# Order-only dependences that put weight splits behind the layer norms, in an fp32 encoder kernel

## Chip, cores and metric

The kernel runs on one core of one Trainium2 chip. The metric is device time in microseconds: 1150.9 us, the median of three runs (1150.8 to 1151.14).

## What is computed

A two-layer encoder over 256 tokens of width 1024, in fp32. Cut to its skeleton:

```python
x = layer_norm(x, emb_ln_g, emb_ln_b)
for l in range(2):
    h = hybrid_mixer(x, ...)            # w_in (1024 x 7680), two attentions, a short convolution, gates, w_mix_out
    x = layer_norm(alpha * x + h, ln_g[l, 0], ln_b[l, 0])
    h = memory_cross_attention(x, mem, ...)   # xa_q, xa_kv (on mem), xa_o
    x = layer_norm(alpha * x + h, ln_g[l, 1], ln_b[l, 1])
    h = conv_ffn(x, ...)                # ffn_w_in (1024 x 5632), convolution, SiLU, ffn_w_out (2816 x 1024)
    x = layer_norm(alpha * x + h, ln_g[l, 2], ln_b[l, 2])
```

So there are seven layer norms: one at the start and three in each layer. Each needs whole rows of the residual, and the next projection needs its result.

## The kernel before

**Weight units.** All weights come as units of 128 x 1024 fp32 numbers (512 KB), in the order in which they are used. `prefetch` (L1063 to L1070) keeps `LOOK = 7` units ahead of the step that is being written: a DMA on SyncE's queue fills a `raw` buffer (four of them), ScalarE rounds it to fp32r (`hi`, the copy of L249), VectorE subtracts (`lo = raw - hi`, L250). `hi` and `lo` have eight buffers each (`WB`). I call the pair of instructions a weight split. A product of two split operands is three matmuls (`mm3`, L244 to L246): high by high, high by low, low by high; a unit feeds 24 of them where it meets 256 tokens.

**Layer norm.** The tokens stand in two tiles of 128 rows, x[0] (x_133 in the printed order) and x[1] (x_134). `ln_part` (L335 to L347) adds the branch's result from PSUM to the residual (L339) and takes statistics of 256 columns (`bn_stats`, L344). `ln` (L349) has two kinds of steps. `norm`: aggregate the statistics (L357), square root on ScalarE (L358), subtract and multiply by the gain (`sub`, L361), reciprocal (L373), scale and add the bias (`scale`, L366; two pieces of 512 columns for x[0], four of 256 for x[1]). `transp`: TensorE transposes a piece into PSUM (L402), then ScalarE and VectorE split it (`split_from`, L249 and L250) into the activations `xt` that the next projection reads.

**Order.** `interleave` lays the steps in one list by hand-written costs, and fill steps (keys and values of the memory, which need no norm) are put where the main line waits. Within that, SyncE's queue keeps the written order; on the other engines a scheduler orders the instructions by its own estimate when the program is built. Each engine then runs its list in order. The PSUM banks `acc` rotate over three buffers, so the third group of a projection reuses the bank of the last key group, which ScalarE copies out (L425). In the cross attention the keys are split too (L250, from a `big` buffer: the key split).

Of the kernel before, what the change touches and what calls it, by code (L numbers as in the profile page):

```python
# [21 lines left out]
AF = mybir.ActivationFunctionType  # L22
ALU = mybir.AluOpType
AX = mybir.AxisListType

P = 128
# [8 lines left out]
ALPHA = (2.0 * DEPTH) ** 0.25  # L35
NEG = -1.0e30
NOSYNC = mybir.DependencyInfo(mybir.DependencyClass.NoSync, mybir.DependencyReason.DATA)
# [75 lines left out]
def interleave(main, fills, banks):  # L113
# [5 lines left out]
    def emit(s):  # L119
        nonlocal clock, free, nfill  # L120
        while nfill < s.fill:
            nfill += 1
            emit(fills[nfill - 1])
        free -= s.acq
        steps.append(s)
        clock += s.cost
        if s.rel:
            pending.append((clock + s.lat, s.rel))

    while cur is not None or active:  # L130
# [4 lines left out]
        for c in list(active):  # L135
            s = c[3]
            if isinstance(s, Spawn):
                active.append([s.name, c[1] + s.delay, s.gen, next(s.gen)])
                c[3] = next(c[2], None)
                moved = True  # L140
            elif s is None:
                done[c[0]] = c[1]
                active.remove(c)
                moved = True
            elif c[1] <= clock and s.acq <= free:
                emit(s)
                c[1] = clock + s.lat
                c[3] = next(c[2], None)
                moved = True
            if moved:  # L150
                break
# [13 lines left out]
        if isinstance(cur, Step) and cur.acq <= free:  # L165
            emit(cur)
            cur = next(main, None)
            continue
# [25 lines left out]
def rd(t):  # L194
    return t.bitcast(F32)


class Encoder:
# [47 lines left out]
        mm(o, ll, rh, start=False, stop=last)  # L246

    def split_from(self, src, ah, al):
        self.nc.scalar.copy(ah, src)  # L249
        self.nc.vector.tensor_tensor(out=al, in0=src, in1=rd(ah), op=ALU.subtract)  # L250

    def proj_f8(self, u, xa, o):

# [80 lines left out]
    def ln_part(self, i, c, acc=None):  # L334

        nc, x = self.nc, self.x[i]
        sl = slice(*c)
        if acc is not None:
            nc.vector.scalar_tensor_tensor(out=x[:, sl], in0=x[:, sl], scalar=ALPHA, in1=acc,  # L339
                                           op0=ALU.mult, op1=ALU.add)  # L340
        if c[0] == 0:
            self.T["st", i] = self.small(24).rearrange("p (c s) -> p c s", c=4)
        for q in range(c[0] // 256, c[1] // 256):
            nc.vector.bn_stats(self.T["st", i][:, q], x[:, 256 * q:256 * q + 256])  # L344
        if i == 0 and c[0] == 0:

            nc.scalar.activation(self.small(1), self.T["st", 0][:, 0, 0:1], AF.Sqrt, bias=self.epsb, scale=0.0)  # L347

    def ln(self, i, nxt, rel, pre=2.6):  # L349

        st = {}
        w = 512 if i == 0 else 256

        def norm():
            nc, x = self.nc, self.x[i]
            mv, rs = self.small(2), self.small(1)
            nc.vector.bn_aggr(mv, self.T["st", i])  # L357
            nc.scalar.activation(rs, mv[:, 1:2], AF.Sqrt, bias=self.epsb, scale=1.0)  # L358
            def sub(h):
                sl = slice(w * h, w * h + w)  # L360
                return nc.vector.scalar_tensor_tensor(out=x[:, sl], in0=x[:, sl], scalar=mv[:, 0:1],  # L361
                                                      in1=self.lng[:, sl], op0=ALU.subtract, op1=ALU.mult)

            def scale(h):
                sl = slice(w * h, w * h + w)
                nc.vector.scalar_tensor_tensor(out=x[:, sl], in0=x[:, sl], scalar=rs,  # L366
                                               in1=self.lnb[:, sl], op0=ALU.mult, op1=ALU.add)

            if nxt is not None:
                for h in range(D // w):  # L370
                    sub(h)
                    if h == 0:
                        nc.vector.reciprocal(rs, rs)  # L373
                    scale(h)
                return

            n, nb = D // w, self.small(1)
            sub(0)
            nc.vector.reciprocal(rs, rs)
            r = nc.vector.scalar_tensor_tensor(out=nb, in0=mv[:, 0:1], scalar=-1.0, in1=rs,  # L380
                                               op0=ALU.mult, op1=ALU.mult)
            sl = slice(w * (n - 1), D)
            nc.scalar.activation(x[:, sl], x[:, sl], AF.Identity, bias=nb, scale=rs)
            nc.gpsimd.tensor_tensor(out=x[:, sl], in0=x[:, sl], in1=self.lng[:, sl], op=ALU.mult)
            nc.gpsimd.tensor_tensor(out=x[:, sl], in0=x[:, sl], in1=self.lnb[:, sl], op=ALU.add)
            for h in range(n - 1):
                if h:
                    self.tc.add_manual_dep(sub(h).ins, r.ins.name, NOSYNC, reason="order of the last rows")
                scale(h)
            for h in range(n):  # L390
                sl = slice(w * h, w * h + w)
                eng = nc.scalar if h % 2 else nc.sync
                eng.dma_start(self.out[i * P:(i + 1) * P, sl], x[:, sl])

        def transp(h):
            nc, n = self.nc, w // P
            if i == 0 and h == 0:
                self.T[nxt] = self.act_tile()
            a = self.T[nxt]
            pt = self.att()[:, :w].rearrange("p (k t) -> p k t", k=n)  # L400
            for k in range(n):
                nc.tensor.transpose(pt[:, k], self.x[i][:, (n * h + k) * P:(n * h + k + 1) * P], self.ident)  # L402
            t, k = n * h // 4, n * h % 4
            self.split_from(pt, a.his[t][:, k:k + n, i * P:(i + 1) * P], a.los[t][:, k:k + n, i * P:(i + 1) * P])

        yield Step(norm, 0, pre, rel=rel)
        if nxt is not None:
            for h in range(D // w):
                yield Step(lambda h=h: transp(h), 0.11 * w / P, 0.3 if h < D // w - 1 else 1.0, acq=1, rel=1)
# [652 lines left out]
    def prefetch(self, upto):  # L1062
        nc = self.nc  # L1063
        while len(self.split) < min(upto, len(self.order)):
            raw = self.raw()
            nc.sync.dma_start(raw, self.aps["w"][len(self.split)])
            hi = self.wp.tile([P, 1024], F32R, tag="hi", name=self.nm("hi"), bufs=self.WB)
            lo = self.wp.tile([P, 1024], F32R, tag="lo", name=self.nm("lo"), bufs=self.WB)
            self.split_from(raw, hi, lo)
            self.split.append((hi, lo))  # L1070

    def load(self, t, src):
# [41 lines left out]
    @with_exitstack  # L1114
    def emit(ctx, self, tc, aps, out):
        nc, PS = tc.nc, bass.MemoryType.PSUM
        self.nc, self.tc, self.aps, self.out = nc, tc, aps, out
        self.uid, self.split, self.bias = 0, [], {}
        self.cst = ctx.enter_context(tc.tile_pool(name="cst", bufs=1))
        self.wp = ctx.enter_context(tc.tile_pool(name="wp", bufs=4))  # L1120
        self.bigp = ctx.enter_context(tc.tile_pool(name="big", bufs=self.BIG))
        self.tmp = ctx.enter_context(tc.tile_pool(name="tmp", bufs=2))
        self.sm = ctx.enter_context(tc.tile_pool(name="sm", bufs=4))
        self.psa = ctx.enter_context(tc.tile_pool(name="psa", bufs=self.ACC, space=PS))
        self.psb = ctx.enter_context(tc.tile_pool(name="psb", bufs=self.ATT, space=PS))
        with tc.manual_schedule(engines={mybir.EngineType.SP}):
            pos = 0
            for s in self.steps:
                if s.units:
                    pos += len(s.units)  # L1130
                    self.prefetch(pos + self.LOOK)
                s.fn(*self.split[pos - len(s.units):pos])
# [59 lines left out]
```

## Time and profile before

| | |
|---|---|
| median of 3 runs | 1150.9 us |
| the profiled execution | 1151.81 us, span 1150.0 us |
| granted TensorE clock, mean | 0.989 |
| TensorE matmul busy | 1114.6 us (97%) |
| VectorE busy | 799.2 us (69%) |
| ScalarE busy | 614.2 us (53%) |
| weight splits on VectorE | 355, 431.8 us, 1222 ns each |
| weight splits on ScalarE | 355, 370.7 us, 1049 ns each |

The busy times are sums over the whole span. Successive instructions of VectorE and ScalarE overlap by some 0.1 us in the records, so n of them take a little less than n times one. [...]

### The profile page before, as it was taken

Reading aid. Unit: us, or ns where it says so; the run is one execution under the profiler, and the core shown is the slowest. Engines: PE = TensorE matmul, PEld = TensorE weight load, DVE = VectorE, ACT = ScalarE, POOL = GpSimd, SP = SyncE. Lnnn points to the kernel's source line nnn. Section 1 sums busy time; section 2 is a strip of 40 time slices with the busy share of each in tenths; the row PEclk is TensorE's granted clock in tenths of the full one; section 3 lists DMA queues with packets and bytes.
Section 4 is the critical chain, followed back from the end, with each engine's and each line's share of the span. In section 5 each row is a group of like instructions: output and inputs, shape, how many; then the busy total and the mean of one; then the engine's idle time right before and its main releaser. Section 6 shows DMA issues by size and latency. Waiting matters only on the chain.

```text
span 1150.0 us, 20250 instructions
## 1 busy us (share of the span) xinstructions
PE 1114.6 (97%) x8172; PEld 1060.7 (92%) x8172; DVE 799.2 (69%) x1198; ACT 614.2 (53%) x958; POOL 12.4 (1%) x18
## 2 busy tenths in 40 slices
PE   7999999999899899999999999999999979999997
PEld 6999999999898899998889999999989969999986
DVE  7788888567764866665586888865696675766644
ACT  6656776444553565554445666654555445555531
POOL 0000000000000000000000000000000000000001
PEclk9999999999899999999999999999999999999999
DMA  7883536456452555555747544555664443555551
GB/s 293 283 257 129 198 115 216 169 195 206 168 184 98 196 183 184 184 183 183 258 146 224 177 149 165 186 174 188 206 232 150 147 155 133 173 183 184 185 181 37
DMA packets 60478, 208.65 MB, mean 181 GB/s; under 512 B 7008, under 2 KB 8288, under 8 KB 60384
## 3 DMA queue, kind: packets, MB, share of 16 engines
q1 hardware_dynamic: 59952, 206.83, 52.7%
q8 instruction: 64, 1.05, 0.4%
q10 hardware_dynamic: 432, 0.52, 0.1%
q14 instruction: 30, 0.25, 0.1%
HBM read 204.18 MB, written 1.05 MB: 178 GB/s over the span
## 4 chain that ended last, share of the span: by engine, by line
PE 68%; DVE 3%; ACT 1%; issue 1%; DMA 0%; DVEq 0%; ACTq 0%
PE acc L245 19%; PE acc L244 19%; PE acc L246 18%; PE att L245 3%; PE att L246 3%; PE att L244 3%; DVE lo L250 1%; PE att L402 1%; DVE x L361 1%; DVE s L344 1%; DVE x L339 0%; DVE x L366 0%; ACT hi L249 0%; DMA raw<-in_w_dram 0%; PE att L603 0%
## 5 line engine op out<-in xcount | busy, mean ns | idle before, releaser
L250 DVE TENSOR_TENSOR lo<-raw,hi 128x1024 fp32r<-128x1024 f32 x355 | 431.8, 1222 | 239.7 <-ACT hi L249 238.1
L249 ACT CAST hi<-raw 128x1024 fp32r<-128x1024 f32 x355 | 370.7, 1049 | 391.4 <-PE acc L245 238.8
L244 PE MATMUL acc<-big,hi 128*128 128x256 f32 x1952 | 556.1, 286 | 3.3 <-ACT big L283 1.7
L245 PE MATMUL acc<-big,hi 128*128 128x256 f32 x1952 | 555.4, 285 | 2.7 <-DVE big L250 2.7
L246 PE MATMUL acc<-big,lo 128*128 128x256 f32 x1952 | 555.3, 285 | 0.2 <-DVE lo L250 0.2
L244 PEld LDWEIGHTS acc<-big,hi 128*128 128x128 f32 x1952 | 375.9, 193 | 5.0 <-ACT big L283 2.1
L245 PEld LDWEIGHTS acc<-big,hi 128*128 128x128 f32 x1952 | 376.2, 193 | 3.4 <-DVE big L250 3.1
L246 PEld LDWEIGHTS acc<-big,lo 128*128 128x128 f32 x1952 | 376.2, 193 | 0.9 <-DVE lo L250 0.7
L244 PE MATMUL acc<-hi,big 128*128 128x512 f32 x296 | 116.8, 398 | 5.3 <-ACT hi L249 5.3
L245 PE MATMUL acc<-lo,big 128*128 128x512 f32 x296 | 117.0, 395 | 0.5 <-DVE lo L250 0.5
L246 PE MATMUL acc<-hi,big 128*128 128x512 f32 x296 | 115.6, 393 | 0.0
L245 PE MATMUL att<-lo,big 128*128 128x256 f32 (+1 forms) x228 | 72.6, 319 | 0.0
L246 PE MATMUL att<-hi,big 128*128 128x256 f32 (+1 forms) x228 | 72.3, 318 | 0.0
L244 PE MATMUL att<-hi,big 128*128 128x256 f32 (+1 forms) x228 | 72.1, 318 | 0.0
L244 PEld LDWEIGHTS acc<-hi,big 128*128 128x128 f32 x296 | 56.1, 190 | 15.2 <-ACT hi L249 5.7
L246 PEld LDWEIGHTS acc<-hi,big 128*128 128x128 f32 x296 | 56.1, 189 | 11.9 <-DVE big L250 0.2
L245 PEld LDWEIGHTS acc<-lo,big 128*128 128x128 f32 x296 | 56.4, 190 | 10.6 <-DVE lo L250 1.2
L250 DVE TENSOR_TENSOR big<-att,big 128x512 fp32r<-128x512 f32 (+2 forms) x64 | 31.8, 518 | 27.3 <-ACT big L249 26.8
L249 ACT CAST big<-att 128x512 fp32r<-128x512 f32 (+2 forms) x64 | 27.9, 454 | 42.4 <-PE att L246 28.6
L244 PEld LDWEIGHTS att<-hi,big 128*128 128x128 f32 x228 | 43.3, 190 | 4.9
L245 PEld LDWEIGHTS att<-lo,big 128*128 128x128 f32 x228 | 43.3, 190 | 4.5
L246 PEld LDWEIGHTS att<-hi,big 128*128 128x128 f32 x228 | 43.3, 190 | 3.0
(143 smaller groups left out, 943.2 us busy)
## 6 DMA issues: line engine op xcount, KB each, us to landing
raw<-in_w_dram SPq DMA_DIRECT2D x355, 512.0 KB, 3.5
t<-in_bias_dram SPq DMA_DIRECT2D x16, 256.0 KB, 4.9
big<-in_ln_g_dram SPq DMA_DIRECT2D x6, 512.0 KB, 6.0
big<-in_ln_b_dram SPq DMA_DIRECT2D x6, 512.0 KB, 6.8
raw<-in_memT_dram SPq DMA_DIRECT2D x6, 512.0 KB, 4.6
big<-big SPq DMA_DIRECT2D x16, 128.0 KB, 2.4
x<-in_x_dram SPq DMA_DIRECT2D x4, 256.0 KB, 7.7
t<-in_memT_dram SPq DMA_DIRECT2D x3, 256.0 KB, 6.5
```

The costliest lines, as they stand in the source:

```text
L244: mm(o, lh, rh, start=first, stop=False)
L245: mm(o, lh, rl, start=False, stop=False)
L246: mm(o, ll, rh, start=False, stop=last)
L249: self.nc.scalar.copy(ah, src)
L250: self.nc.vector.tensor_tensor(out=al, in0=src, in1=rd(ah), op=ALU.subtract)
L344: nc.vector.bn_stats(self.T["st", i][:, q], x[:, 256 * q:256 * q + 256])
L361: return nc.vector.scalar_tensor_tensor(out=x[:, sl], in0=x[:, sl], scalar=mv[:, 0:1], in1=self.lng[:, sl], op0=ALU.subtract, op1=ALU.mult)
L402: nc.tensor.transpose(pt[:, k], self.x[i][:, (n * h + k) * P:(n * h + k + 1) * P], self.ident)
```

## The change

`split_from` now returns its two instructions. `urgent` remembers, for each engine, the last instruction of a layer norm; `behind` gives a weight split an order-only dependence (`NOSYNC`: it orders two instructions of one engine's list, with no semaphore and no wait) on it. A weight split that is written after a norm's step may thus no longer be placed ahead of that step on VectorE or ScalarE. Weight splits written before it, and other instructions, are free as before.

```diff
     def split_from(self, src, ah, al):
-        self.nc.scalar.copy(ah, src)
-        self.nc.vector.tensor_tensor(out=al, in0=src, in1=rd(ah), op=ALU.subtract)
+        return (self.nc.scalar.copy(ah, src),
+                self.nc.vector.tensor_tensor(out=al, in0=src, in1=rd(ah), op=ALU.subtract))
+
+    def urgent(self, ins):
+
+        self.ahead[ins.ins.engine] = ins.ins.name
+        return ins
+
+    def behind(self, ins):
+        name = self.ahead.get(ins.ins.engine)
+        if name is not None:
+            self.tc.add_manual_dep(ins.ins, name, NOSYNC, reason="behind a layer norm")
...
-            nc.scalar.activation(rs, mv[:, 1:2], AF.Sqrt, bias=self.epsb, scale=1.0)
+            self.urgent(nc.scalar.activation(rs, mv[:, 1:2], AF.Sqrt, bias=self.epsb, scale=1.0))
...
-                    scale(h)
+                    self.urgent(scale(h))
...
-            self.split_from(pt, a.his[t][:, k:k + n, i * P:(i + 1) * P], a.los[t][:, k:k + n, i * P:(i + 1) * P])
+            for ins in self.split_from(pt, a.his[t][:, k:k + n, i * P:(i + 1) * P],
+                                       a.los[t][:, k:k + n, i * P:(i + 1) * P]):
+                self.urgent(ins)
...
-            self.split_from(raw, hi, lo)
+            for ins in self.split_from(raw, hi, lo):
+                self.behind(ins)
```

The residual add (L339) and `bn_stats` (L344) of `ln_part` are marked `urgent` in the same way.

The order moves at six of the seven norms: on VectorE 41 rows and on ScalarE 33 of the order before stand elsewhere or are cut otherwise, and TensorE's list follows; SyncE's and GpSimd's lists are the same. Three places follow. In the rows `lo_n<-raw,hi` and `hi_n<-raw` are the two halves of a weight split, `big<-att,big` and `big<-att` those of a transposed piece of the norm, `big_3606<-big_288` a key split; lines of the changed kernel are 10 to 13 higher (L344 is L354, L357 is L367, L361 is L372, L366 is L377, L425 is L438).

VectorE at the norm after the mixer of layer 0, from the last statistics of x_134 on. Before:

```order
L344 BN_STATS s_3311<-x_134 128x6
L250 TENSOR_TENSOR lo_3456<-raw_3453,hi_3455 128x1024
L250 TENSOR_TENSOR lo_3494<-raw_3491,hi_3493 128x1024
L357 BN_AGGR s_3440<-s_3311 128x2
L250 TENSOR_TENSOR lo_3530<-raw_3527,hi_3529 128x1024
L250 TENSOR_TENSOR big_3431<-att_3433,big_3429 128x4x128
L361 SCALAR_TENSOR_TENSOR x_134<-x_134,s_3440,big_3214 128x256 x4
L250 TENSOR_TENSOR big_3432<-att_3484,big_3430 128x4x128
L373 RECIPROCAL s_3441<-s_3441 128x1
L250 TENSOR_TENSOR lo_3566<-raw_3563,hi_3565 128x1024
L250 TENSOR_TENSOR big_3606<-big_288,big_3604 128x1024
L366 SCALAR_TENSOR_TENSOR x_134<-x_134,s_3441,big_3215 128x256 x4
```

and with the change:

```order
L367 BN_AGGR s_3440<-s_3311 128x2
L372 SCALAR_TENSOR_TENSOR x_134<-x_134,s_3440,big_3214 128x256 x4
L384 RECIPROCAL s_3441<-s_3441 128x1
L377 SCALAR_TENSOR_TENSOR x_134<-x_134,s_3441,big_3215 128x256 x2
L250 TENSOR_TENSOR big_3431<-att_3433,big_3429 128x4x128
L377 SCALAR_TENSOR_TENSOR x_134<-x_134,s_3441,big_3215 128x256 x2
L250 TENSOR_TENSOR lo_3456<-raw_3453,hi_3455 128x1024
L250 TENSOR_TENSOR big_3432<-att_3484,big_3430 128x4x128
L250 TENSOR_TENSOR lo_3494<-raw_3491,hi_3493 128x1024
L250 TENSOR_TENSOR big_3606<-big_288,big_3604 128x1024
L250 TENSOR_TENSOR big_3431<-att_3522,big_3429 128x2x128
L250 TENSOR_TENSOR lo_3530<-raw_3527,hi_3529 128x1024
```

The norm's arithmetic closes up, and the weight splits move in between the splits of the transposed pieces.

ScalarE at the same norm, before:

```order
L249 CAST hi_3529<-raw_3527 128x1024
L249 CAST big_3429<-att_3433 128x4x128
L249 CAST big_3430<-att_3484 128x4x128
L358 ACTIVATE s_3441<-s_3440,epsb 128x1
L425 COPY big_289<-acc_3459 128x512
L249 CAST hi_3565<-raw_3563 128x1024
L249 CAST big_3604<-big_288 128x1024
L249 CAST hi_3614<-raw_3612 128x1024
L425 COPY big_289<-acc_3533 128x512
L249 CAST big_3605<-big_289 128x1024
L249 CAST big_3429<-att_3522 128x2x128
```

and with the change:

```order
L368 ACTIVATE s_3441<-s_3440,epsb 128x1
L249 CAST hi_3455<-raw_3453 128x1024
L249 CAST big_3429<-att_3433 128x4x128
L249 CAST big_3430<-att_3484 128x4x128
L249 CAST hi_3493<-raw_3491 128x1024
L438 COPY big_289<-acc_3459 128x512
L249 CAST big_3604<-big_288 128x1024
L249 CAST big_3429<-att_3522 128x2x128
L249 CAST hi_3529<-raw_3527 128x1024
L249 CAST big_3429<-att_3558 128x2x128
L249 CAST hi_3565<-raw_3563 128x1024
L438 COPY big_289<-acc_3533 128x512
```

The square root and the pieces of the norm moved ahead of weight casts; the copy that frees the bank of acc_3533, which stood ahead of the pieces att_3522 and att_3558, now stands behind both and behind two weight casts between and after them.

VectorE at the start norm, before:

```order
L366 SCALAR_TENSOR_TENSOR x_133<-x_133,s_173,big_157 128x512 x2
L366 SCALAR_TENSOR_TENSOR x_134<-x_134,s_182,big_157 128x256 x3
L250 TENSOR_TENSOR lo_197<-raw_194,hi_196 128x1024
L366 SCALAR_TENSOR_TENSOR x_134<-x_134,s_182,big_157 128x256
L250 TENSOR_TENSOR lo_203<-raw_200,hi_202 128x1024
```

and with the change:

```order
L377 SCALAR_TENSOR_TENSOR x_133<-x_133,s_173,big_157 128x512 x2
L377 SCALAR_TENSOR_TENSOR x_134<-x_134,s_182,big_157 128x256 x4
L250 TENSOR_TENSOR lo_197<-raw_194,hi_196 128x1024
L250 TENSOR_TENSOR lo_203<-raw_200,hi_202 128x1024
L250 TENSOR_TENSOR lo_223<-raw_220,hi_222 128x1024
```

The fourth scaling of x_134 went ahead of the split lo_197, whose unit TensorE is about to read.

## Rows read from the trace of the kernel before

**Rows 1.** The page, parts 1 and 4: busy time of the engines, and the engines' shares of the chain that ended last.

```profile
PE 1114.6 (97%) x8172; PEld 1060.7 (92%) x8172; DVE 799.2 (69%) x1198; ACT 614.2 (53%) x958; POOL 12.4 (1%) x18
...
PE 68%; DVE 3%; ACT 1%; issue 1%; DMA 0%; DVEq 0%; ACTq 0%
```

**Rows 2.** Table of stretches: from and to in us, length, busy time of PE, PEld, DVE, ACT and POOL with counts, granted TensorE clock, DMA share, GB/s.

```profile
300.00:330.00 30.00, 26.08 (x193) 25.25 (x192) 17.29 (x28) 14.72 (x23) 0.00 (x0) 0.89 0.37 131
380.00:410.00 30.00, 26.72 (x212) 26.29 (x211) 22.32 (x37) 14.67 (x22) 0.00 (x0) 0.94 0.53 176
615.00:850.00 235.00, 233.18 (x1833) 227.16 (x1832) 175.93 (x259) 137.25 (x229) 1.89 (x2) 1.00 0.53 182
850.00:880.00 30.00, 28.28 (x179) 25.76 (x178) 22.12 (x33) 14.48 (x21) 0.00 (x0) 0.94 0.53 177
925.00:985.00 60.00, 52.31 (x348) 48.41 (x347) 42.00 (x70) 30.55 (x45) 0.00 (x0) 0.94 0.46 158
```

**Rows 3.** Timeline of TensorE at the norm after the mixer of layer 0: start and length in us, engine, line, operation, operands, form, count, and in brackets the idle time before it and what ended it.

```profile
303.53 1.23 PE L402 MATMUL att<-ident,x 128*128 128x128 f32 x6 [1.94 <-DVE x L366]
...
307.32 0.58 PE L245 MATMUL acc<-big,hi 128*128 128x256 f32 x1 [1.98 <-DVE big L250]
...
312.97 0.28 PE L244 MATMUL acc<-big,hi 128*128 128x256 f32 x1
313.09 0.28 PE L245 MATMUL acc<-big,hi 128*128 128x256 f32 x1
```

**Rows 4.** Timeline of VectorE at the same norm (columns as in rows 3).

```profile
293.94 2.34 DVE L250 TENSOR_TENSOR lo<-raw,hi 128x1024 fp32r<-128x1024 f32 x2
296.20 0.25 DVE L357 BATCH_NORM_AGGREGATE s<-s 128x2 f32<-128x24 f32 x1
...
297.88 0.68 DVE L250 TENSOR_TENSOR big<-att,big 128x512 fp32r<-128x512 f32 x1
298.48 1.66 DVE L361 SCALAR_TENSOR_TENSOR x<-x,s,big 128x256 f32<-128x256 f32 x4
...
302.99 1.67 DVE L366 SCALAR_TENSOR_TENSOR x<-x,s,big 128x256 f32<-128x256 f32 x4
...
306.85 1.41 DVE L250 TENSOR_TENSOR big<-att,big 128x256 fp32r<-128x256 f32 x4
```

**Rows 5.** Timeline of ScalarE at the same norm.

```profile
297.24 1.27 ACT L249 CAST big<-att 128x512 fp32r<-128x512 f32 x2 [0.53 <-PE att L402]
...
298.60 0.58 ACT L425 COPY big<-acc 128x512 f32<-128x512 f32 x1
299.06 1.06 ACT L249 CAST hi<-raw 128x1024 fp32r<-128x1024 f32 x1
300.01 1.06 ACT L249 CAST big<-big 128x1024 fp32r<-128x1024 f32 x1
```

**Rows 6.** Waits of TensorE between 615 and 850 us: engine and line, what it waited for, us in total, times, longest us.

```profile
PE acc L244 <- ACT big L283: 1.2, 1, 1.2
```

**Rows 7.** Timeline of TensorE at the norm after the cross attention of layer 0.

```profile
394.79 1.54 PE L402 MATMUL att<-ident,x 128*128 128x128 f32 x6 [3.28 <-DVE x L366]
...
397.05 0.56 PE L245 MATMUL acc<-big,hi 128*128 128x256 f32 x1
```

**Rows 8.** Timeline of VectorE there.

```profile
384.19 1.21 DVE L250 TENSOR_TENSOR lo<-raw,hi 128x1024 fp32r<-128x1024 f32 x1
...
387.82 1.41 DVE L366 SCALAR_TENSOR_TENSOR x<-x,s,big 128x512 f32<-128x512 f32 x2
...
394.26 1.66 DVE L366 SCALAR_TENSOR_TENSOR x<-x,s,big 128x256 f32<-128x256 f32 x4
```

**Rows 9.** Timeline of VectorE at the norm after the mixer of layer 1.

```profile
853.12 2.34 DVE L250 TENSOR_TENSOR lo<-raw,hi 128x1024 fp32r<-128x1024 f32 x2
...
859.88 0.15 DVE L373 RECIPROCAL s<-s 128x1 f32<-128x1 f32 x1
...
861.14 1.67 DVE L366 SCALAR_TENSOR_TENSOR x<-x,s,big 128x256 f32<-128x256 f32 x4
```

**Rows 10.** Timeline of TensorE there.

```profile
867.89 0.62 PE L244 MATMUL acc<-big,hi 128*128 128x256 f32 x3 [1.02 <-ACT big L249]
869.21 0.57 PE L245 MATMUL acc<-big,hi 128*128 128x256 f32 x1 [0.70 <-DVE big L250]
```

**Rows 11.** Timeline of TensorE at the norm after the FFN of layer 0.

```profile
597.65 1.23 PE L402 MATMUL att<-ident,x 128*128 128x128 f32 x6 [0.28 <-DVE x L366]
```

**Rows 12.** Timeline of VectorE at the norm after the cross attention of layer 1.

```profile
945.17 1.21 DVE L250 TENSOR_TENSOR lo<-raw,hi 128x1024 fp32r<-128x1024 f32 x1
```

**Rows 13.** Timeline of TensorE there and at the start of the FFN that follows.

```profile
947.38 1.09 PE L402 MATMUL att<-ident,x 128*128 128x128 f32 x4 [7.29 <-DVE x L366]
...
973.60 0.39 PE L244 MATMUL acc<-big,hi 128*128 128x256 f32 x1 [0.41 <-DVE fa L1017]
```

**Rows 14.** Timeline of VectorE at the start norm.

```profile
27.64 1.21 DVE L250 TENSOR_TENSOR lo<-raw,hi 128x1024 fp32r<-128x1024 f32 x1
28.77 0.47 DVE L366 SCALAR_TENSOR_TENSOR x<-x,s,big 128x256 f32<-128x256 f32 x1
```

**Rows 15.** Timeline of TensorE there.

```profile
28.91 0.38 PE L246 MATMUL acc<-big,lo 128*128 128x256 f32 x1 [0.23 <-DVE lo L250]
```

**Rows 16.** Waits over the whole span (columns as in rows 6).

```profile
ACT hi L249 <- PE acc L245: 238.8, 167, 8.4
```

More of the change, by code (lines that the diff above doesn't have):

```diff
@@ L338, in ln_part @@
         if acc is not None:
-            nc.vector.scalar_tensor_tensor(out=x[:, sl], in0=x[:, sl], scalar=ALPHA, in1=acc,
-                                           op0=ALU.mult, op1=ALU.add)
+            self.urgent(nc.vector.scalar_tensor_tensor(out=x[:, sl], in0=x[:, sl], scalar=ALPHA, in1=acc,
+                                                       op0=ALU.mult, op1=ALU.add))
         if c[0] == 0:
@@ L343, in ln_part @@
         for q in range(c[0] // 256, c[1] // 256):
-            nc.vector.bn_stats(self.T["st", i][:, q], x[:, 256 * q:256 * q + 256])
+            self.urgent(nc.vector.bn_stats(self.T["st", i][:, q], x[:, 256 * q:256 * q + 256]))
         if i == 0 and c[0] == 0:
@@ L365, in scale @@
                 sl = slice(w * h, w * h + w)
-                nc.vector.scalar_tensor_tensor(out=x[:, sl], in0=x[:, sl], scalar=rs,
-                                               in1=self.lnb[:, sl], op0=ALU.mult, op1=ALU.add)
+                return nc.vector.scalar_tensor_tensor(out=x[:, sl], in0=x[:, sl], scalar=rs,
+                                                      in1=self.lnb[:, sl], op0=ALU.mult, op1=ALU.add)
             if nxt is not None:
@@ L1117, in emit @@
         self.nc, self.tc, self.aps, self.out = nc, tc, aps, out
-        self.uid, self.split, self.bias = 0, [], {}
+        self.uid, self.split, self.bias, self.ahead = 0, [], {}, {}
         self.cst = ctx.enter_context(tc.tile_pool(name="cst", bufs=1))
```

## Prediction

> **What bounds the kernel now.** I read the page first: TensorE is busy 97% of the span, and in the chain that ended last it has 68%, VectorE 3%, ScalarE 1% [rows 1]. So there is little to win, and it lies where TensorE stands still. The table of stretches says where: in four of the five rows the granted clock is under 1.00, and all four of these have 1.7 to 7.7 us without a matmul (length less TensorE's busy time) [rows 2]. Each holds the layer norm that ends a mixer or a cross attention. I call them mixer norm 0 (300 to 330 us), cross norm 0 (380 to 410), mixer norm 1 (850 to 880) and cross norm 1 (925 to 985); FFN norm 0 lies near 597 and the start norm near 28. The timeline of each engine then shows what the norm waits for. The reader should see in it that VectorE is not waiting: it works through weight splits of about 1.17 us each while the norm's next operation stands behind them.
>
> **Mixer norm 0.** TensorE has nothing from 301.59 to 303.53, and again before 307.32, 3.92 us in all [rows 3]. [...]
> In the new order the four weight splits and the key split that stood between the last statistics and the last scaling come later. VectorE starts at 293.94 with the norm: aggregate 0.25, four subtractions 1.66, reciprocal (smaller still), two of the four scalings 0.84 (half of 1.67): 296.8 [rows 4]. The split of x_133's first transposes (x_133 and x_134 are the two halves of the tokens) is not ready before 297.88 and takes 0.68; two scalings follow, so x_134 is ready at 299.3 instead of 304.66 [rows 4]. Then come, in the printed order, two weight splits, a 512-wide split and a key split (3 x 1.17 + 0.6) and the first 256-wide one (0.35, a quarter of 1.41): 303.8.
> ScalarE is later. Its two casts end at 298.5; then a weight cast 0.95 (299.06 to 300.01), a copy 0.46, the key cast 1.0, and two 256-wide casts (0.35 each, about half of a 512-wide one) with two weight casts between: 303.5 [rows 5]. Only then comes the copy that frees the bank of key group acc_3533 (0.58), which the third matmul after the transposes needs: 304.1. That copy is the new last wait; the first matmul that reads a low half (below: the low-half matmul) starts at 304.3 instead of 307.32, worth 3.0. Its clock term is 0 to 2.5: TensorE keeps one gap of about 1.2 us. A wait of 1.2 us in the stretch from 615 to 850 left the clock at 1.00 [rows 2, 6], the nearest row, so I take the 2.5. Sum 5.5, ends 3.0 and 6.4 (all of 3.9 and 2.5).
> [...]
>
> **Cross norm 0.** TensorE stops at 391.51 and the first low-half matmul is at 397.05 [rows 7]. Without the splits VectorE goes from 384.19 through reciprocal and aggregate (0.4), two scalings (1.41), four subtractions (1.66 as before), four scalings (1.66): x_134 is ready by 389.4 instead of 395.92 [rows 8], before TensorE needs it. Behind it two weight splits and two 512-wide splits (2 x 1.17 + 2 x 0.6), then a 256-wide one: 393.3. So 3.8 earlier, less 0.3 since the second 256-wide cast stands behind another weight cast: 3.5, ends 2.0 (the clock still falls and costs the 1.6 of mixer norm 1) and 4.8.
>
> **Mixer norm 1.** The norm of x_134 starts at 853.12 and is through at 856.9 (0.25 + 1.67 + 0.15 + 1.67), not at 862.8 [rows 9]. Its transposes now stand between value matmuls, and the splits (five weights 5.9, two of 0.6, four of 0.35) end near 866.5 with a microsecond of waiting, as TensorE arrives at 866.87. It no longer waits until 869.21 [rows 10]: 2.0 after the two matmuls done early. The clock row of 0.94 over 30 us is 3.6 us at half speed [rows 2], at mixer norm 0's rate (2.5 per 5.77) 1.6. Sum 3.6, ends 2.0 and 3.7.
>
> **The small ones.** FFN norm 0: two splits go, and the wait of 0.28 with them [rows 11]; 0.3. Cross norm 1: one split of 1.21 goes [rows 12], of a TensorE gap of 7.29 [rows 13]; 1.1 earlier, but the work that gains it runs in the half-clock stretch, so 0.6, ends 0.5 and 1.1. Its next limit is x_133's arithmetic, which no split holds. Start norm: the last scaling (0.47) now stands ahead of a weight split that TensorE already waits 0.23 for [rows 14, 15]: a loss of 0.4. Last, the order at cross norm 0 puts the first SiLU behind more casts; the bank it frees is where cross norm 1 already has a wait of 0.41 [rows 13]: I take another 0.4 lost, ends 0 and 1. The final norm has no splits behind it. DMA issues keep their order; a held split keeps its raw buffer up to some 5 us longer, which the lead (below) covers.
>
> **Sum.** 5.5 + 3.5 + 3.6 + 0.3 + 0.6 - 0.4 - 0.4 = 12.7 us. The profiled execution took 1151.81 (span 1150.0), 0.9 above the median of 1150.9; it would be 1139.1, and the median **1138.2**.
>
> **Rivals.**
> A, the clock falls all the same at mixer norm 0 and cross norm 0. For it: at mixer norm 1 two gaps of 1.02 and 0.70 were followed by half speed [rows 10]. Against: the 1.2 us wait above. The gain is 12.7 - 2.5 - 1.6 = 8.6: 1142.3. [...]
> B, VectorE is the bound: the same splits must run, and TensorE needs the last 256-wide one. Behind 303.8 stand two weight splits and three 256-wide ones, so it would end at 307.2 instead of 308.26 [rows 4], worth 1.1, as much again at cross norm 0, with 2.0, 0.3 and 0.6 elsewhere less 0.8: 4.3, 1146.6. Against: TensorE's new order runs three groups on the first features while the rest arrive.
> C, slower, by starving. Held splits start later by about 5.3 (mixer norm 0), 4.8, 4.8, 3.6 and 7, 25.5 us together. If TensorE ran out of split units it would pay that, less 12.7: 1163. It decides once a hold outlasts the units already split. Against: ScalarE waits 238.8 us, 167 times, for TensorE to free a weight buffer [rows 16]: the buffers are normally full, and three units (24 matmuls of 0.12, 2.9 us each) lie ready at cross norm 0.
> D, nothing: the engines' queues already let the norm by in time. The waits there [rows 3, 7] name the norm's own operations, so hardly: 1151.
>
> **Numbers.** Forecast 0.59, A 0.22, B 0.10, C 0.05, D 0.04. No change means within 0.2% (2.3 us), about what a measurement of this kernel can tell. Faster 0.91, same 0.04, slower 0.05. The range holds the forecast's ends (1134.4 with all upper ones) and rival A with a microsecond to spare: 1134.0 to 1143.5.
>
> **What would show it.** VectorE should run the four scalings of x_134 near 299, 389 and 856 (less what was gained earlier), with no 1024-wide split between the last statistics and them. TensorE's gap should be near 1.2 at mixer norm 0 with a ScalarE copy as its releaser, under 1 at cross norm 0, none at mixer norm 1, about 6.2 at cross norm 1; the granted clock 1.00 in the first three. I am wrong if TensorE waits for weight splits (lo from raw) after a norm, if the low-half matmuls wait for the 256-wide splits as long as before, or if the clock still falls at all four.

## The result and the profile after

The changed kernel takes **1138.1 us** (median, 1137.3 to 1140.1) against 1150.9 (1150.1 to 1151.1): a ratio of 0.9888, 95% interval 0.9872 to 0.9905. The forecast was 1138.2, in a range of 1134.0 to 1143.5. The profiled execution took 1137.27 (span 1135.5) and lies 0.9 below its median, as that of before lay 0.9 above its own. So the two traces differ by 14.5 us where the medians differ by 12.7, and the terms read from the traces have to add up to 14.5.

The page after, busy line and chain of waits, beside [rows 1]:

```profile
PE 1107.2 (98%) x8172; PEld 1055.0 (93%) x8172; DVE 799.4 (70%) x1198; ACT 611.8 (54%) x958; POOL 12.4 (1%) x18
...
PE 94%; DVE 2%; ACT 2%; issue 1%; DMA 1%; SPq 0%; DVEq 0%; ACTq 0%
```

VectorE and ScalarE do the same work as before. TensorE is busy for 7.4 us less with as many instructions. That is mostly time at the lower clock, in which a matmul counts as busy for longer: in the trace of before the granted clock is 0.50 (half speed) from 307 to 312 us, with matmuls of 0.41 us that start 0.21 apart, and 1.00 from 313 on, with matmuls of 0.28 that start 0.12 apart. It is 0.50 too from 395 to 398, from 870 to 872 and from 945 to 951, and in the trace after from 930 to 936. By the granted clocks in [rows 2] the first three norms lost 0.11, 0.06 and 0.06 of 30 us, 6.9 us by this estimate, and lose none now. The stretches (columns as in [rows 2]) show it; the four norms come earlier now, so they are cut elsewhere:

```profile
290.00:330.00 40.00, 38.62 (x324) 38.41 (x323) 31.66 (x48) 22.57 (x33) 0.00 (x0) 1.00 0.55 185
372.00:405.00 33.00, 32.67 (x272) 32.28 (x271) 27.04 (x46) 18.57 (x27) 0.00 (x0) 1.00 0.58 192
...
840.00:870.00 30.00, 30.00 (x210) 27.76 (x209) 25.82 (x36) 17.31 (x24) 0.00 (x0) 1.00 0.63 214
915.00:975.00 60.00, 53.39 (x367) 49.86 (x366) 44.79 (x75) 33.05 (x49) 0.00 (x0) 0.94 0.47 161
```

Of these four norms, the granted clock is 1.00 at the first three and under it (0.94) at cross norm 1 alone. Length less busy time leaves 1.38, 0.33 and 0 us where there were 3.92, 3.28 and 1.72.

TensorE at these places, beside [rows 3, 7, 10, 13]:

```profile
302.42 0.28 PE L246 MATMUL acc<-big,lo 128*128 128x256 f32 x1
302.55 0.60 PE L413 MATMUL att<-ident,x 128*128 128x128 f32 x4
302.90 0.48 PE L244 MATMUL acc<-big,hi 128*128 128x256 f32 x2
304.76 0.39 PE L244 MATMUL acc<-big,hi 128*128 128x256 f32 x1 [1.38 <-ACT big L438]
304.99 0.28 PE L245 MATMUL acc<-big,hi 128*128 128x256 f32 x1
...
387.90 0.62 PE L244 MATMUL acc<-big,hi 128*128 128x256 f32 x3 [0.33 <-ACT big L249]
...
933.08 1.09 PE L413 MATMUL att<-ident,x 128*128 128x128 f32 x4 [6.20 <-DVE x L377]
```

The wait of 1.38 stands before the third matmul after the transposes, and what ended it is the copy of the key group (line 438 now). The last matmul ahead of those transposes, at 302.42, ends at 302.70. VectorE at mixer norm 0, beside [rows 4]:

```profile
294.27 0.42 DVE L354 BATCH_NORM_STATS2 s<-x 128x6 f32<-128x256 f32 x1
...
296.81 0.88 DVE L377 SCALAR_TENSOR_TENSOR x<-x,s,big 128x256 f32<-128x256 f32 x2
...
299.14 0.87 DVE L377 SCALAR_TENSOR_TENSOR x<-x,s,big 128x256 f32<-128x256 f32 x2
299.93 1.22 DVE L250 TENSOR_TENSOR lo<-raw,hi 128x1024 fp32r<-128x1024 f32 x1
...
303.94 0.42 DVE L250 TENSOR_TENSOR big<-att,big 128x256 fp32r<-128x256 f32 x1
```

The first weight split after the statistics starts at 299.93, behind the last scaling. ScalarE there, beside [rows 5]:

```profile
301.95 1.05 ACT L249 CAST hi<-raw 128x1024 fp32r<-128x1024 f32 x1
302.91 0.37 ACT L249 CAST big<-att 128x256 fp32r<-128x256 f32 x1
303.17 1.05 ACT L249 CAST hi<-raw 128x1024 fp32r<-128x1024 f32 x1
304.12 0.59 ACT L438 COPY big<-acc 128x512 f32<-128x512 f32 x1
```

The copy stands behind two weight casts: it starts at 304.12, 1.4 us after the matmul that ends at 302.70, and ends at 304.71; TensorE goes on at 304.76.

Where the 14.5 us came from is read by following equal instructions through both traces. These are the starts of ScalarE's table load at each norm's first statistics (it comes before the norm's own waits), and of TensorE's resumption at cross norm 1:

| place | before | after | offset | since the row above |
|---|---|---|---|---|
| mixer norm 0 | 276.0 | 276.7 | +0.7 | +0.7 (start) |
| cross norm 0 | 374.8 | 370.0 | -4.8 | -5.5 (mixer norm 0) |
| FFN norm 0 | 575.3 | 566.3 | -9.0 | -4.2 (cross norm 0) |
| mixer norm 1 | 835.1 | 825.6 | -9.5 | -0.5 (FFN norm 0) |
| cross norm 1 | 935.8 | 922.6 | -13.2 | -3.7 (mixer norm 1) |
| resumption at cross norm 1 | 947.38 | 933.08 | -14.3 | -1.1 (cross norm 1) |
| end of the span | 1150.0 | 1135.5 | -14.5 | -0.2 |

### The profile page after: what moved, and what is told of

Same layout as the page of the kernel before. It is cut to its first block, busy times and chain, and to the rows that moved or that the text cites. A ratio compares the mean times of both kernels' runs of the same rounds, so it can differ in the third digit from the quotient of the medians.

```text
span 1135.5 us, 20248 instructions
## 1 busy us (share of the span) xinstructions
PE 1107.2 (98%) x8172; PEld 1055.0 (93%) x8172; DVE 799.4 (70%) x1198; ACT 611.8 (54%) x958; POOL 12.4 (1%) x18
## 4 chain that ended last, share of the span: by engine, by line
PE 94%; DVE 2%; ACT 2%; issue 1%; DMA 1%; SPq 0%; DVEq 0%; ACTq 0%
PE acc L244 26%; PE acc L245 26%; PE acc L246 26%; PE att L245 4%; PE att L246 4%; PE att L244 4%; ACT hi L249 1%; PE att L413 1%; PE att L616 1%; PE att L531 1%; DVE lo L250 1%; DMA raw<-in_w_dram 1%; PE att L530 1%; DVE x L372 1%; DVE x L377 0%
```

## Experiments

**One norm alone.** Are the terms separate? The marks are set only while between 91 and 99 units have been issued, which is around mixer norm 0.

```
     def urgent(self, ins):
-        self.ahead[ins.ins.engine] = ins.ins.name
+        if 91 <= len(self.split) <= 99:
+            self.ahead[ins.ins.engine] = ins.ins.name
         return ins
```

> The marks are set at mixer norm 0 alone; everywhere else the splits stand as before. Theory (the terms are separate, and this one is 5.5): offsets of equal instructions in the two traces put 5.5 us of the gain on this norm, so 1150.9 - 5.5 = 1145.4, a ratio of 0.9952; TensorE's last wait there is about 1.4 us on a ScalarE copy and the granted clock is 1.00, while at cross norm 0 and mixer norm 1 the gaps and the lower clock of before are still there. Rival, VectorE-bound (rival B of the prediction): 1.1 us, 1149.8. Rival, the gain is only moved on to the next norm: under 3 us, over 1147.9.

Measured: 1147.0 (nine runs, 1144.3 to 1151.4), a ratio of 0.9961 (0.9947 to 0.9976), which is 2.8 to 6.1 us: it holds the 5.5, excludes 1.1 and does not quite exclude the second rival's 3. The trace does: the wait at mixer norm 0 is again 1.38 on the copy, the table load of mixer norm 0 is at 276.4 (+0.5) and that of cross norm 0 at 369.6 (-5.2), so 5.7 us are gained at this norm, and at the next norm none of it is lost again. One part of the expectation failed. TensorE at cross norm 0, and the stretches from 290 us on, around cross norm 0 and around mixer norm 1:

```profile
389.51 1.23 PE L414 MATMUL att<-ident,x 128*128 128x128 f32 x6 [3.22 <-DVE x L378]
```

```profile
290.00:330.00 40.00, 38.62 (x324) 38.42 (x323) 31.55 (x48) 22.16 (x33) 0.00 (x0) 1.00 0.57 186
380.00:400.00 20.00, 16.78 (x139) 16.16 (x138) 13.97 (x26) 9.34 (x15) 0.00 (x0) 1.00 0.51 167
850.00:880.00 30.00, 28.28 (x190) 26.25 (x189) 20.77 (x31) 15.01 (x22) 0.00 (x0) 0.94 0.50 162
```

At cross norm 0 the wait is as long as before (3.22, and 3.28 in [rows 7]), but the clock is 1.00, and the next norm is another 1.3 us earlier for it. A wait of that length did not fix the clock here. At mixer norm 1 the lower clock is there as expected.

**Without the start norm's marks.** No mark is set before more than 18 units have been issued, which is after the start norm.

```
-        self.ahead[ins.ins.engine] = ins.ins.name
+        if len(self.split) > 18:
+            self.ahead[ins.ins.engine] = ins.ins.name
```

> All marks of the change but those of the start norm. Theory: the start norm's marks cost 0.4 us (a wait of 0.62 where before had 0.23), so 1137.7 beside the change's 1138.1, and the wait near 29 us reads 0.23 again. Rival: the 0.7 us by which the changed kernel was behind at 88 us is all variation of the first transfers: 1138.1, and the position at 88 us differs as much as before. A difference of 0.4 is at the edge of what the times can tell; the wait in the trace decides.

Measured: 1137.7, ratio 0.9879 (0.9864 to 0.9895); the times cannot tell 0.4. The trace can:

```profile
29.14 0.39 PE L246 MATMUL acc<-big,lo 128*128 128x256 f32 x1 [0.23 <-DVE lo L250]
```

0.23 as in [rows 15], where the changed kernel waits 0.62. At 304.31 TensorE is 0.45 ahead of the changed kernel (304.76). The term of 0.4 is right. The other 0.3 by which the changed kernel was late at mixer norm 0 is not traced to a cause; it is within what executions with 8 buffers and without these marks differ by there (their table loads start between 276.0 and 276.6).

**One engine's half of the order.** Both halves of a split were held. Which one matters? The first added line below is one run, the second the other.

```
     def behind(self, ins):
         name = self.ahead.get(ins.ins.engine)
-        if name is not None:
+        if name is not None and ins.ins.engine == mybir.EngineType.DVE:
+        if name is not None and ins.ins.engine == mybir.EngineType.Activation:
```

> Only VectorE's half of each weight split goes behind the norm; ScalarE's casts of weights stand where the scheduler puts them, up to three of them ahead of the norm's square root. Theory 1 (VectorE's queue is what made the norm late; the casts find free buffers): the square root comes some 1 to 2 us later than in the changed kernel but the copy that ends the wait at mixer norm 0 stands behind the same casts, so 1139 to 1140. Theory 2 (ScalarE's casts wait for TensorE to free a weight buffer, and the norm's square root stands behind them): the scalings of x_134 are 2 to 5 us later at three norms, and half or more of the gain is lost: 1144 or more.

> Only ScalarE's half of each weight split (the cast) goes behind the norm. A subtraction on VectorE needs its cast, so by the order one weight split instead of four stands between x_134's last statistics and its last scaling at mixer norm 0. Theory (a cast held is a split held): one split of 1.2 us each at mixer norm 0 and cross norm 0, so 1139 to 1141. Rival (only an order on VectorE itself lets the norm through): most of the gain is lost, 1146 or more.

Measured: VectorE alone 1138.25 (ratio 0.9881, 0.9866 to 0.9896), ScalarE alone 1137.5 (0.9879, 0.9865 to 0.9893). Either half gives the whole gain; for VectorE's I had expected 1 to 2 us less, for ScalarE's 1 to 3. Theory 2 of the first and the rival of the second fall, and the small losses of the two theories did not come either. With VectorE's half alone, the square root does come later at mixer norm 0, and VectorE waits for it:

```profile
297.38 0.29 ACT L368 ACTIVATE s<-s,epsb 128x1 f32<-128x1 f32 x1
```

```profile
297.71 0.16 DVE L384 RECIPROCAL s<-s 128x1 f32<-128x1 f32 x1 [0.96 <-ACT s L368]
```

It started at 295.03 in the changed kernel. But there VectorE stood idle for 0.84 us a little later, before the split that starts at 298.54; in this run it does not, and x_134 is ready at 300.2 instead of 300.0. What is left there is a wait of TensorE of 0.76 on VectorE. With ScalarE's half alone one weight split stands ahead of the scalings, as expected (at 296.33), and falls into the same idle time, so here the held casts held their subtractions at no cost (1137.5, where both halves held gave 1138.1). ScalarE in that run, at mixer norm 0:

```profile
301.94 0.59 ACT L438 COPY big<-acc 128x512 f32<-128x512 f32 x1 [0.74 <-PE acc L246]
302.43 0.38 ACT L249 CAST big<-att 128x256 fp32r<-128x256 f32 x1
302.69 1.06 ACT L249 CAST hi<-raw 128x1024 fp32r<-128x1024 f32 x1
```

Here the copy stands ahead of the casts and waits for TensorE, and no wait of TensorE over 0.3 us is left there. With the trace of the changed kernel, where TensorE resumes 0.05 us after the copy ends, this says that the 1.38 is the copy's place in the queue. (At cross norm 0 this run waits 0.81 instead of 0.33, which takes half a microsecond back.)

**The key splits behind the norm too.** On top of the run without the start norm's marks:

```
     def split_keys(self, l):
...
-            self.split_from(src[t], hi[t], lo[t])
+            for ins in self.split_from(src[t], hi[t], lo[t]):
+                self.behind(ins)
```

> The change without the start norm's marks, and with the splits of the memory keys (two casts and two subtractions of 1024 columns, whose result the first cross-attention head needs 20 us later) behind the norm too, like weight splits. Theory (the wait of 1.38 at mixer norm 0 is ScalarE's queue ahead of the copy of acc_3533): one cast of 1.0 fewer stands ahead of the copy, and one subtraction of 1.2 fewer ahead of the first 256-wide one, so the wait falls to 0.3 to 0.5 and the time by 1.0 against the run without the start norm's marks: 1136.7. Rival (the split of the last weights or VectorE is the limit): the wait stays over 1.2 with VectorE as its releaser. Rival (the scores of the first head now wait for the key split): a wait on it near 325 us takes the 1.0 back.

Measured: 1136.1 (1135.8 to 1137.2), ratio 0.9867 (0.9852 to 0.9882). TensorE and ScalarE:

```profile
302.15 0.60 PE L414 MATMUL att<-ident,x 128*128 128x128 f32 x4
302.51 0.48 PE L244 MATMUL acc<-big,hi 128*128 128x256 f32 x2
302.88 0.39 PE L245 MATMUL acc<-big,hi 128*128 128x256 f32 x1
```

```profile
302.77 1.06 ACT L249 CAST hi<-raw 128x1024 fp32r<-128x1024 f32 x1
303.72 0.59 ACT L439 COPY big<-acc 128x512 f32<-128x512 f32 x1
```

The wait is gone, but not as I expected: the copy is no earlier. In the run that this one builds on it is

```profile
303.67 0.59 ACT L439 COPY big<-acc 128x512 f32<-128x512 f32 x1
```

Where the key cast stood, ScalarE now waits 1.07 us for transposes. Still the copy stands behind both weight casts. What moved is VectorE's first 256-wide split, from 303.48 to 302.41, and in TensorE's order the first group's low-half matmul (302.88) now stands before the third group's first one, so nothing needs the copy's bank until later. From 193 to 636 us this run gains 1.4 on the one it builds on. No wait for the key split appears.

**The clock of the kernel before, once more** (the kernel unchanged).

> The kernel before, once more, for its granted clock. With the marks at mixer norm 0 alone, cross norm 0 kept its gap of 3.2 us, yet the granted clock there read 1.00 instead of 0.91. Theory (a gap of this size brings the lower clock in some executions, depending on what lies before it): half speed is seen at some of the four norms, not always with the same lengths, and the time moves by its cost (1.3 to 2.5 us each). Rival (the gap fixes it): half speed at all four norms again, with 0.91 from 380 to 410 us or the same number of microseconds.

Measured: 1150.4, profiled with a span of 1148.6 where [rows 1] had 1150.0. The stretches of [rows 2], and TensorE at mixer norm 1:

```profile
300.00:330.00 30.00, 26.47 (x198) 25.48 (x197) 17.85 (x28) 15.06 (x23) 0.00 (x0) 0.89 0.42 145
380.00:410.00 30.00, 26.78 (x215) 26.35 (x214) 22.09 (x36) 15.09 (x23) 0.00 (x0) 0.94 0.56 179
850.00:880.00 30.00, 28.28 (x192) 25.76 (x190) 23.38 (x35) 16.11 (x23) 0.00 (x0) 1.00 0.56 191
```

```profile
867.66 0.62 PE L244 MATMUL acc<-big,hi 128*128 128x256 f32 x3 [1.02 <-ACT big L249]
868.98 0.39 PE L245 MATMUL acc<-big,hi 128*128 128x256 f32 x1 [0.70 <-DVE big L250]
```

Mixer norm 1 has the same two waits as in [rows 10], to the hundredth, with the clock at 1.00 instead of 0.94. So half speed there belongs to single executions. The rival (the gap fixes it) falls. From the table load of mixer norm 1 to that of cross norm 1 this execution takes 99.1 us instead of 100.7: the lower clock costs 1.6 there.

**Fewer weight buffers**, before and after: when does a held split starve TensorE?

```
-    LOOK = 7
+    LOOK = 4
-    WB = 8
+    WB = 5
```

> The kernel before with 5 weight buffers instead of 8 and a lead of 4 units instead of 7. Four units are held by the second half of an output projection, so one unit instead of four lies ready behind it. Theory: some waits of TensorE for weight splits behind mixer norm 0, cross norm 0 and mixer norm 1, 1155 to 1175. If splits are never late even so, 1151.

> The changed kernel with the same 5 buffers and a lead of 4 units. Theory (rival C of the prediction decides once a hold outlasts the units already split; one unit is 2.9 us of matmuls, a hold some 5): behind each norm TensorE now waits for the held split, so the gain against the kernel before with 5 buffers shrinks from 12.7 to 6 or less, or turns into a loss of up to 10. Rival (a hold costs nothing at any lead, since the norm is what TensorE waits for): the gain stays at 10 to 14.

Measured: before 1150.5 (ratio 0.9987, 0.9976 to 0.9998), after 1144.1 (0.9933, 0.9915 to 0.9951): the gain shrinks from 12.7 to 6.4. The 1155 to 1175 expected for the kernel before did not come. For the changed one the number is near what I expected, but by luck: the reason is another. The kernel before with 5 buffers at mixer norm 0, then the changed one:

```profile
305.05 1.23 PE L402 MATMUL att<-ident,x 128*128 128x128 f32 x6 [0.87 <-DVE x L366]
307.98 0.44 PE L402 MATMUL att<-ident,x 128*128 128x128 f32 x2 [0.95 <-DVE big L250]
308.91 0.38 PE L245 MATMUL acc<-big,hi 128*128 128x256 f32 x1 [0.49 <-DVE big L250]
```

```profile
306.40 0.39 PE L245 MATMUL acc<-big,hi 128*128 128x256 f32 x1 [0.81 <-DVE big L250]
307.70 0.39 PE L244 MATMUL acc<-big,hi 128*128 128x256 f32 x1 [0.32 <-ACT big L438]
```

With fewer buffers fewer splits stand ahead of the norm (three weight splits between x_134's last statistics and its last scaling, not four and a key split), so the kernel before already waits less (2.31 instead of 3.92). Over the first three norms with waits (mixer 0, cross 0, mixer 1) these waits come to 4.55 us before and 2.27 after; with 8 buffers they were 8.92 and 1.71. So what the change saves in these waits falls from 7.2 to 2.3 us, most of the 6.3 by which the gain shrinks. In neither run does TensorE wait for a weight split behind these norms. Starving has not been shown even with one unit ready. The small lead costs the changed kernel 6 us; both runs with 5 buffers are some 1.9 us behind their counterparts by 195 us already, ahead of these norms, and the cause of the rest stays open.

**The splits that were issued before the marks.** At cross norm 1 the changed kernel still waits 6.20 us. VectorE there:

```profile
922.09 1.40 DVE L354 BATCH_NORM_STATS2 s<-x 128x6 f32<-128x256 f32 x4
923.41 1.21 DVE L250 TENSOR_TENSOR lo<-raw,hi 128x1024 fp32r<-128x1024 f32 x1
...
926.12 1.21 DVE L250 TENSOR_TENSOR lo<-raw,hi 128x1024 fp32r<-128x1024 f32 x1
...
928.03 2.35 DVE L250 TENSOR_TENSOR lo<-raw,hi 128x1024 fp32r<-128x1024 f32 x2
930.29 1.41 DVE L372 SCALAR_TENSOR_TENSOR x<-x,s,big 128x512 f32<-128x512 f32 x2
...
932.25 1.34 DVE L377 SCALAR_TENSOR_TENSOR x<-x,s,big 128x512 f32<-128x512 f32 x2
```

Four weight splits stand between x_133's first statistics and its subtractions. They were issued before the norm, when no mark of it existed, so the change cannot hold them. On top of the run with the key splits held:

```
-                    self.prefetch(pos + self.LOOK)
+                    self.prefetch(293 if 293 - self.LOOK < pos <= 290 else pos + self.LOOK)
```

> The run with the key splits held, and now the four weight splits that are issued just ahead of cross norm 1 are issued after it (while the units are at 287 to 290, no split beyond the 293rd is issued), so that they too find the norm's marks and go behind it. In the trace of the changed kernel these four (1.21, 1.21, 2.35 us) stand on VectorE between x_133's first statistics and its subtractions. Theory (they, not the norm's own arithmetic, make the 6.20 us wait of TensorE): the first scaling ends 4.5 to 5 us earlier, the wait falls to 1 to 2 us, and the time by 4.5 to 5 (1131.4), by up to 3 more if the lower clock goes with it. Rival 1, the sentence of the prediction (x_133's own arithmetic is the limit, which no split holds): the wait stays at 5 to 6. Rival 2 (starving, rival C at a place where it has fewer units ready): a wait of 2 us or more for a weight split takes its place behind the norm, and the gain is under 2.

> The changed kernel once more, beside the run above on the same chip: 1138.1, a ratio of 0.989 to the kernel before; its trace again with a wait of about 1.4 at mixer norm 0 on a ScalarE copy and of 6.2 at cross norm 1, half speed at cross norm 1 alone. If half speed turns up at another norm too, it belongs to single executions and not to the order of the work.

Measured: **1130.6** (1130.2 to 1132.5), ratio to before 0.9830 (0.9815 to 0.9845), and the changed kernel on the same chip 1138.4, 0.9891 (0.9874 to 0.9907), with its waits of 1.38 and 6.20 again and the lower clock at cross norm 1 alone of the four norms (0.69 from 930 to 935 us, 0.63 from 935 to 940). VectorE, TensorE and the stretch in the run with the cap:

```profile
923.77 0.24 DVE L368 BATCH_NORM_AGGREGATE s<-s 128x2 f32<-128x24 f32 x1
924.05 1.42 DVE L373 SCALAR_TENSOR_TENSOR x<-x,s,big 128x512 f32<-128x512 f32 x2
...
925.77 1.41 DVE L378 SCALAR_TENSOR_TENSOR x<-x,s,big 128x512 f32<-128x512 f32 x2
...
932.37 4.62 DVE L250 TENSOR_TENSOR lo<-raw,hi 128x1024 fp32r<-128x1024 f32 x4
```

```profile
926.66 0.63 PE L414 MATMUL att<-ident,x 128*128 128x128 f32 x4 [1.39 <-DVE x L378]
```

```profile
915.00:975.00 60.00, 57.38 (x414) 53.62 (x413) 48.99 (x80) 35.44 (x54) 0.00 (x0) 1.00 0.55 183
```

The first scaling starts 6.5 us earlier (some 1.6 of it gained at earlier norms), the wait falls to 1.39 from 6.20, which is what the run that this one builds on has there too, and the clock stays at 1.00. Rivals 1 and 2 fall: the four splits made the wait, and run later (932.37) without making TensorE wait for them: behind the norm its longest waits are 0.40, on a VectorE split into `big`, and 0.73, where the FFN that follows waited 0.41 before. This version beats both kernels: 20 us below before, 7.8 below the changed one.

## Why the prediction was right, and where it was not

**What bounds the kernel** held: VectorE, working through splits in the order of its queue, was what TensorE waited for. VectorE's and ScalarE's busy times are within 0.5% of before, and the table puts the gain at the norms.

**Mixer norm 0**, 5.5: 5.5 by the table, 5.7 with this norm alone. The steps hold too: x_134 ready at 299.3 was forecast, 300.0 measured, which is the 0.7 of the start; the copy was to end at 304.1 and ended at 304.71. The 304.1 has the copy wait for everything that the printed order puts ahead of it on ScalarE, and that is what the trace shows: the copy stands behind two casts and starts 1.4 us after the matmul that ends at 302.70, where ScalarE's half alone puts it ahead of them and the wait is gone. What the wait also needs is TensorE's own order: with the key splits held the copy is still behind the casts, but other matmuls stand first and nothing waits. No run shows the clock's 2.5 by itself; what the trace of before shows in its place is 27 matmuls from 307.32 to 313.09, 5.77 us where 27 at 0.12 apart take 3.24, and in the changed kernel the clock is 1.00 there.

**Cross norm 0**, 3.5: 4.2. The wait went from 3.28 to 0.33, 2.9; the other 1.3 is the clock alone, as the run with one norm shows. The term was too small because it stops at the first low-half matmul, which came 3.9 earlier (388.36, plus the 4.8, for 397.05): the lower clock held on behind it before (0.50 from 397 to 398 us, 0.89 from 398 to 399), and only the term's lower end had a price for that. x_134 was ready at 384.4, the forecast's 389.4 less the 4.8 gained earlier.

**Mixer norm 1**, 3.6: 3.7, no wait left. x_134 is ready at 847.4, the forecast's 856.9 less the 9.5 gained earlier. About 1.6 of the 3.7 is the clock, though, and the second run of the kernel before is an execution that does not pay it (99.1 us to the next norm instead of 100.7). The term is right for the profiled execution and too large for one that keeps its clock there.

**The small ones.** FFN norm 0: 0.3, measured 0.5. Start norm: -0.4, confirmed by its wait. SiLU: -0.4, measured nothing (no wait over 0.2 us has come up in the FFN behind cross norm 0, and the 0.41 behind cross norm 1 is 0.41 still). Cross norm 1: 0.6, measured 1.3, the 1.09 by which the wait is shorter (7.29 to 6.20) and 0.2 behind it; that half of it would be lost at half clock was wrong, since the shorter wait counts in full.

**The sum**: 12.7 forecast, 12.7 between the medians, 14.5 between the traces. That the medians agree to a tenth is partly luck: the terms in the traces were under-sized by 1.8 (cross norm 0 and cross norm 1 by 0.7 each, SiLU by 0.4), and the profiled executions lay 0.9 above and 0.9 below their medians. In the traces TensorE's waits at the norms are 8.6 us shorter; most of the other 6 is the clock (2.5, 1.3 and 1.6 at the first three norms, an estimate from [rows 3], the run with one norm and the second run of the kernel before), which other executions of the kernel before pay only in part. Two smaller sums of the prediction are off, and nothing hangs on them: all upper ends together give 15.9 us and 1135.0, not 1134.4, and rival C comes to 1163.7.

**The step that failed**, in a prediction that held otherwise, is the sentence that x_133's arithmetic limits cross norm 1 and no split holds it. Four did: holding them took 4.8 us off the wait. I had compared where splits went, and taken those that did not move for no part of the limit; the run with the cap shows that they were all of the wait but 1.4 us.

**Rivals.** A: the clock did not fall at the first three norms (1.00) in either profiled execution of the change, behind waits of up to 1.38. But its ground was half right: the same waits of 1.02 and 0.70 at mixer norm 1 went with the lower clock in [rows 2] (0.94) and with 1.00 in the second run of the kernel before, and at cross norm 0 a wait of 3.28 went with 0.94 and one of 3.22 with 1.00. So the lower clock can come with such waits; the runs do not bear out that it must. B (VectorE the bound, 1.1 at mixer norm 0) is excluded by 5.7. C (starving) did not happen: behind the six norms after the start norm no wait of TensorE over 0.2 us was for a weight split, even at 5 buffers. D is excluded by the interval.

## What to carry to other kernels

An order-only dependence on the last instruction of a critical chain paid here (1150.9 to 1138.1), where background work stood ahead of the chain in the same engine's list, but it holds only what is issued after the mark: look for background work issued just ahead of the chain, and move its issue too. Here either engine's half of the order was enough. After such a move, list what in the queue now stands ahead of each copy that frees a PSUM bank; that was the next wait at mixer norm 0.

## What the runs showed of the hardware

The granted clock was not a function of the wait before it: the kernel before, run twice, had 0.94 and 1.00 at mixer norm 1 behind identical waits, and the run with mixer norm 0 alone 0.94 behind the same two; behind 3.2 to 3.3 us at cross norm 0 the same three executions had 0.94, 0.94 and 1.00. Much of the scatter of one kernel goes with it. Of 34 executions of the kernel before beside these experiments, those with a mean granted clock of 0.991 or more over the span took 1148.9 to 1151.6 us, those at 0.988 or less 1152.8 to 1155.8 (0.003 of 1150 us is 3.5, so the sizes agree); the run with mixer norm 0 alone went from 1144.3 (0.995) to 1151.4 (0.989). So for this kernel a term for the clock is best given as a range that starts at nothing.
